# Seven-product projections that alternate between PSUM banks, with PSUM tiles of two banks, and attention transposes behind all value blocks

## The chip, the cores and the metric

The kernel runs on one core of one Trainium2 chip. The metric is the device time of one execution, in microseconds; lower is better. The engines are named as the profile names them: PE is TensorE (PEld its weight loads), ACT is ScalarE, DVE is VectorE, POOL is GpSimd, SP is SyncE, which here issues DMAs. PSUM, where products are summed, has banks of 512 fp32 values in each of 128 partitions.

## What is computed

One decoder layer in fp32 with D = 1024, 512 tokens and 16 meta tokens ahead of them (whose output is dropped). Two attention branches, retention with 4 heads and gated linear attention (GLA) with 4 heads, share one input projection, and sigmoid gates merge them:

```python
u = rms_norm(h, norm_gain)
proj = u @ w_in                      # 1024 x 11280 columns
(rq, rk, rv, rg, gq, gk, gv, gg, glr, m_ret, m_gla) = jnp.split(proj, points, axis=-1)
...
rq, rk = rope(rq), rope(rk) * 256 ** -0.5            # 4 heads of 256
o_ret = retention_chunked(rq, rk, rv)                # values: 4 heads of 512
o_ret = head_group_norm(o_ret, ret_norm_gain) * silu(rg)
...
o_gla = gla_chunked(gq, gk, gv, log_a)
o_gla = head_rms_norm(o_gla, gla_norm_gain) * silu(gg)
merged = sigmoid(m_ret) * (o_ret @ w_branch_ret) + sigmoid(m_gla) * (o_gla @ w_branch_gla)
return rms_norm(h + merged @ w_out, final_norm_gain)
```

(`rope` rotates the halves: `t1*cos - t2*sin` and `t2*cos + t1*sin`.)

## The kernel before

**Products.** Each fp32 operand is split in a rounded high part and the rest (`split`, lines 140 and 141: ACT casts to `hi`, DVE subtracts to `lo`), and each product is three matmuls: high by high, high by low, low by high. A weight is 512 x 256 in SBUF (`[128, 4, 256]`); its split has one cast on ACT and one subtraction on DVE. The splits lie in pools of three buffers each (`wsplit`).

**`quad`** computes two blocks of 256 columns of a projection from a 2 x 2 blocking with seven products in place of eight. The sums of activations (`fh`, `fl`, forms A11 to S4) are made once, those of weights at each quad on DVE (`tensor_sub` on `blk`, and `t2`). A product is 24 matmuls (2 halves, 4 pieces of 128, 3 parts). The products gather in three places, a, b and c. The order is 1 to b, 2 to a, 7 to c, then 6, 5 and 3 each added to b, then 4 to c. Bank b is copied by ACT to SBUF (`copy`, line 228) after product 1 (x1), after 6 (x2) and after 5 (x3), because the later products add to it; results are a + x1, c + x3, b, and c + x2. There are 21 quads. Those named `gq` and `rq` (query and key) are wide: the tokens with the meta tokens are the moving side, 264 columns for each half, so that a, b and c have two banks each. The others (`gg`, `gv1`, `rg`, `rv`, and the gates `mr`, `mg`) have 256 columns for each half and one bank each.

**PSUM.** Eight banks: pool `pp` with four tiles of one bank (b and c of the quads, the sums of branches and of the output), pool `pa` with four (a of the wide quads, attention, transposes).

**Evacuation.** The function `evac` that `quad` is given is called for each result; in wide quads for each of the two banks apart. For `rq` it applies `rope`: four multiplications on DVE, a subtraction and an addition on POOL (lines 757 to 762), and two splits.

**Attention of retention** (`ret_attention`): `values(ib)` for each block of 128 tokens computes a block of outputs `av` and norms it on DVE, POOL and ACT to gated rows `sg` (line 874). `turn` transposes `sg` on TensorE for two blocks at a time (line 337, tiles `ot`) and splits the result to `oh` (ACT) and `ol` (DVE). The order is values 0, 1, 2, turn 0, values 3, turn 1. `branch` multiplies `oh`, `ol` by the output weights (tiles `br_p`, eight sums of 512 columns, 12 matmuls each), each sum added to `acc2` by DVE.

**What sets the order.** The generators are woven: `weave(dense, chain)` advances the attention chain by one step after each product. Heads: `rq` of head h is woven with attention of head h-1, then comes the branch of head h-1, `rg` is woven with the scores, then `rv`. The gates are woven with attention of head 3. A scheduler then lays out each engine's instructions one after the other in one list, which need not be the order written; each engine goes through its list in order and waits at semaphores.

Of the kernel before, what the change touches and what calls it, by code (L numbers as in the profile page):

```python
# [106 lines left out]
def hybrid_kernel(ctx: ExitStack, tc: tile.TileContext, I, out: bass.AP):  # L107
# [6 lines left out]
    pp = ctx.enter_context(tc.tile_pool(name="pp", bufs=4, space=PSUM))  # L114
# [18 lines left out]
    def ppt(name):  # L133
        return pp.tile([P, 512], F32, tag="pp", name=name)
# [51 lines left out]
    def quad(cols, rows, name, evac, meta=None, wide=False):  # L186
# [13 lines left out]
        n_tok = HT if wide else 512  # L200
        banks = {}

        def bank(x):
            banks[x] = [(pat if wide and x == "a" else ppt)(f"{name}_{x}{t}") for t in range(2 if wide else 1)]

        def product(i, form, w, x, fresh):
            hi, lo = wsplit([P, 4, 256], f"{name}_{i}")
            split(hi, lo, w)
            if fresh:
                bank(x)  # L210
            for t in range(2):
                ps = banks[x][t][:, :HT] if wide else banks[x][0][:, t * 256:(t + 1) * 256]
                c = slice(t * P, (t + 1) * P)
                for kk in range(4):
                    a = [f[form][:, kk, c] if rows else f[form][:, kk, :HT if wide else 256] for f in (fh, fl)]
                    b = [f[:, kk, :] if rows else f[:, kk, c] for f in (hi, lo)]
                    first = fresh and kk == 0 and (wide or t == 0)
                    last = kk == 3
                    for j, (x1, x2) in enumerate(((0, 0), (0, 1), (1, 0))):
                        l, r = (a[x1], b[x2]) if rows else (b[x1], a[x2])  # L220
                        nc.tensor.matmul(ps, l, r, start=first and j == 0, stop=last and j == 2,  # L221
                                         skip_group_check=not fresh or (t == 1 and not wide))

        def copy(x, n):

            y = xc.tile([P, 2, HT] if wide else [P, 512], F32, tag="xc", name=f"{name}_x{n}")
            for t in range(2 if wide else 1):
                nc.scalar.copy(y[:, t, :] if wide else y, banks[x][t][:, :n_tok])  # L228
            return y

        def out(n, th, x, y):
            for t in range(2 if wide else 1):
                p = banks[x][t][:, :n_tok]
                q = y[:, t, :] if y is not None and wide else y
                evac(n, th, t if wide else None, p, q)
# [10 lines left out]
        x1 = copy("b", 1)  # L246
# [4 lines left out]
        nc.vector.tensor_sub(blk[0, 0], blk[0, 1], blk[0, 0])  # L251
# [30 lines left out]
    def proj_b(src, col, left, name, evac, meta=None):  # L282

        pss = [ppt(f"{name}_p{t}") for t in range(NTB)]
# [31 lines left out]
    def branch(src, row0, oh, ol, name, evac):  # L316
        for q in range(4):
# [3 lines left out]
            split(hi, lo, raw)  # L321
            for cc in range(2):
                c = 2 * q + cc
                ps = ppt(f"{name}_p{c}")
                for k in range(4):
                    mm3(ps, hi[:, k, cc * P:(cc + 1) * P], lo[:, k, cc * P:(cc + 1) * P], oh[:, k, :], ol[:, k, :],
                        k == 0, k == 3)
                evac(c, ps)
                yield
# [179 lines left out]
    def total(dst, p, q):  # L509
        if q is None:  # L510
            nc.scalar.copy(dst, p)
        else:
            nc.vector.tensor_add(dst, p, q)

    def pair(x):
        return x if x is None else x.rearrange("p (t c) -> p t c", t=2)

    def rows_into(dst, func=None):
        def f(n, th, t, p, q):
            d = dst[:, 2 * th:2 * th + 2, n * 256:(n + 1) * 256]  # L520
            if func is None:
                total(d, pair(p), pair(q))
                return
            if q is not None:
                total(d, pair(p), pair(q))
            nc.scalar.activation(d, pair(p) if q is None else d, func)
# [26 lines left out]
    def gla_qk(p):  # L553
# [4 lines left out]
        def evac(n, th, t, x, y):  # L558
            if n == 1:
                total(k[:, t, th, :], x, y)  # L560
            else:
                total(q[:, t, th * 256:(th + 1) * 256], x[:, :256], y if y is None else y[:, :256])
# [152 lines left out]
    def gla_branch(p):  # L715
        def evac(c, ps):
            if p == 0:
                nc.scalar.copy(acc[:, c, :], ps)
            else:
                nc.vector.tensor_add(acc[:, c, :], acc[:, c, :], ps)  # L720
                nc.sync.dma_start(kept[:, c, :], acc[:, c, :])
# [26 lines left out]

    def tmp(name):
        return rp.tile([P, 512], F32, tag="tmp", name=name, bufs=6)  # L750

    def rope(ts, th, dst, name):

        n = ts[0].shape[-1]
        co, si = cs[:, 0, th, :n], cs[:, 1, th, :n]
        m = [tmp(f"{name}_{i}")[:, :n] for i in range(4)]
        nc.vector.tensor_mul(m[0], ts[0], co)
        nc.vector.tensor_mul(m[1], ts[1], si)
        nc.gpsimd.tensor_sub(m[0], m[0], m[1])
        nc.vector.tensor_mul(m[2], ts[1], co)  # L760
        nc.vector.tensor_mul(m[3], ts[0], si)
        nc.gpsimd.tensor_add(m[2], m[2], m[3])
        for i in range(2):
            split(dst[0][i], dst[1][i], m[2 * i])

    def ret_qk(h):
# [5 lines left out]
        held = {}  # L772

        def evac(n, th, t, x, y):
            w = HT if n else 256
            if y is not None:
                s = tmp(f"qs{h}{n}{th}{t}")
                nc.vector.tensor_add(s[:, :w], x[:, :w], y[:, :w])
                x = s
            held[n, th, t] = x[:, :w]  # L780
            if t == 1:
                if n:
                    dst = [[f[:, i, th, :] for i in range(2)] for f in (kh, kl)]
                else:
                    dst = [[f[:, i, th * 256:(th + 1) * 256] for i in range(2)] for f in (qh, ql)]
                rope((held[n, th, 0], held[n, th, 1]), th, dst, f"rp{h}{n}{th}")
# [11 lines left out]
    def ret_v(h):  # L798
# [11 lines left out]
        def evac(n, th, t, x, y):  # L810
            x = pair(x)
            if y is not None:
                s = pair(tmp(f"vs{h}{n}{th}"))
                nc.vector.tensor_add(s, x, pair(y))
# [36 lines left out]
    def ret_attention(h):  # L851
# [39 lines left out]
    def gate(dst, n, th, p, q):  # L891
        if q is not None:
            nc.vector.tensor_add(dst, pair(p), pair(q))
        nc.scalar.activation(dst, pair(p) if q is None else dst, AF.Sigmoid)

    def gates():
# [3 lines left out]
        def evac_ret(j):  # L900
            def f(n, th, t, p, q):
                s = slice(th * 256, (th + 1) * 256)
                g = sigr[2 * j + n][:, :, s]
                gate(g, n, th, p, q)
# [4 lines left out]
        def evac_gla(j):  # L909
            def f(n, th, t, p, q):  # L910
                s = slice(th * 256, (th + 1) * 256)
                d = slice(4 * j + 2 * n, 4 * j + 2 * n + 2)
                k = pair(tmp(f"kp{j}{n}{th}"))
                nc.sync.dma_start(k, kept[:, d, s])
                g = pair(tmp(f"mg{j}{n}{th}"))
# [121 lines left out]
```

## Time and profile before

| | |
|---|---|
| time, median of 3 runs | 840.84 us (840.45 to 843.05) |
| the profiled execution | 841.58 us, its span 839.8 us |
| mean granted clock of TensorE | 0.988 |
| PE busy | 784.0 us (93%) |
| DVE busy | 619.5 us (74%) |
| ACT busy | 422.8 us (50%) |
| POOL busy | 133.7 us (16%) |
| DMA | 78.82 MB, mean 94 GB/s |

The span is the time from the first to the last instruction of the profiled execution; 1.8 us of its time lie around it. A matmul's record lasts longer than the distance to the next one, since matmuls are pipelined, so busy shares of PE overstate how well it is used: idle time is read from the waits and from the distance between starts.

### The profile page before, as it was taken

Reading aid. Unit: us, or ns where it says so; the run is one execution under the profiler, and the core shown is the slowest. Engines: PE = TensorE matmul, PEld = TensorE weight load, DVE = VectorE, ACT = ScalarE, POOL = GpSimd, SP = SyncE. Lnnn points to the kernel's source line nnn. Section 1 sums busy time; section 2 is a strip of 40 time slices with the busy share of each in tenths; the row PEclk is TensorE's granted clock in tenths of the full one; section 3 lists DMA queues with packets and bytes.
Section 4 is the critical chain, followed back from the end, with each engine's and each line's share of the span. In section 5 each row is a group of like instructions: output and inputs, shape, how many; then the busy total and the mean of one; then the engine's idle time right before and its main releaser. Section 6 shows DMA issues by size and latency. Waiting matters only on the chain. (4 is left out here: it accounts for less than half of the span.)

```text
span 839.8 us, 13348 instructions
## 1 busy us (share of the span) xinstructions
PE 784.0 (93%) x5322; PEld 703.9 (84%) x5322; DVE 619.5 (74%) x893; ACT 422.8 (50%) x707; POOL 133.7 (16%) x170
## 2 busy tenths in 40 slices
PE   7987989999899989999999999999999998989996
PEld 4777888898787978987999879998799998888886
DVE  3889686777637698887677887788877877887822
ACT  6665775456742445545445443454434555454422
POOL 4500332022400130022000220002200000032031
PEclk8998999999999999999999999999999999999999
DMA  8212211224122504242222422224222236335202
GB/s 278 84 56 76 76 45 54 66 90 126 52 75 100 177 25 127 77 125 75 69 81 79 126 76 64 81 83 127 76 64 82 82 105 208 114 103 176 73 1 101
DMA packets 72390, 78.82 MB, mean 94 GB/s; under 512 B 6964, under 2 KB 64564, under 8 KB 72328
## 3 DMA queue, kind: packets, MB, share of 16 engines
q1 hardware_dynamic: 72328, 77.97, 30.5%
q8 instruction: 42, 0.69, 0.3%
q14 instruction: 20, 0.16, 0.1%
HBM read 73.77 MB, written 4.19 MB: 93 GB/s over the span
## 5 line engine op out<-in xcount | busy, mean ns | idle before, releaser
L152 POOL TENSOR_TENSOR g_r<-g_v,mhalf 128x1 f32<-128x1 f32 x16 | 10.1, 630 | 305.7 <-DVE g_v L151 305.7
L144 PE MATMUL br_p<-oh,br_h 128*128 128x512 f32 x128 | 50.7, 401 | 1.0 <-ACT br_h L140 1.0
L145 PE MATMUL br_p<-ol,br_h 128*128 128x512 f32 x128 | 50.3, 396 | 0.0
L146 PE MATMUL br_p<-oh,br_l 128*128 128x512 f32 x128 | 50.1, 395 | 0.0
L140 ACT CAST rg_h<-rg_w 128x1024 fp32r<-128x1024 f32 x24 | 25.3, 1052 | 45.8 <-PE br_p L145 24.2
L140 ACT CAST rq_h<-rq_w 128x1024 fp32r<-128x1024 f32 x24 | 25.3, 1053 | 34.4 <-PE bg_p L145 13.0
L221 PE MATMUL rv_b<-rv_h,fh 128*128 128x256 f32 x128 | 37.0, 289 | 3.5 <-ACT rv_x L228 3.5
L221 PE MATMUL rq_b<-fh,rq_h 128*128 128x264 f32 x128 | 36.9, 288 | 1.0 <-ACT rq_x L228 1.0
L141 DVE TENSOR_TENSOR rg_l<-rg_w,rg_h 128x1024 fp32r<-128x1024 f32 x24 | 29.3, 1221 | 11.3 <-ACT rg_h L140 11.3
L221 PE MATMUL rg_b<-rg_h,fh 128*128 128x256 f32 x128 | 36.6, 286 | 0.9 <-DVE rp L760 0.9
L221 PE MATMUL rq_b<-fh,rq_l 128*128 128x264 f32 x128 | 36.6, 286 | 0.0
L221 PE MATMUL rq_b<-fl,rq_h 128*128 128x264 f32 x128 | 36.3, 283 | 0.0
L221 PE MATMUL rv_b<-rv_l,fh 128*128 128x256 f32 x128 | 36.0, 281 | 0.0
L221 PE MATMUL rg_b<-rg_l,fh 128*128 128x256 f32 x128 | 36.0, 281 | 0.0
L221 PE MATMUL rv_b<-rv_h,fl 128*128 128x256 f32 x128 | 36.0, 281 | 0.0
L221 PE MATMUL rg_b<-rg_h,fl 128*128 128x256 f32 x128 | 35.9, 281 | 0.0
L141 DVE TENSOR_TENSOR rv_l<-rv_w,rv_h 128x1024 fp32r<-128x1024 f32 x24 | 29.0, 1222 | 8.0 <-ACT rv_h L140 7.8
L141 DVE TENSOR_TENSOR rq_l<-rq_w,rq_h 128x1024 fp32r<-128x1024 f32 x24 | 30.4, 1266 | 3.9 <-ACT rq_h L140 3.9
L140 ACT CAST rv_h<-rv_w 128x1024 fp32r<-128x1024 f32 x24 | 24.8, 1053 | 12.2 <-DVE rv_w L252 5.6
L144 PEld LDWEIGHTS br_p<-oh,br_h 128*128 128x128 f32 x128 | 23.8, 188 | 8.2 <-ACT br_h L140 1.2
L221 PEld LDWEIGHTS rv_b<-rv_h,fh 128*128 128x128 f32 x128 | 24.1, 188 | 7.3 <-ACT rv_x L228 6.1
L145 PEld LDWEIGHTS br_p<-ol,br_h 128*128 128x128 f32 x128 | 24.1, 188 | 5.9
(478 smaller groups left out, 3062.1 us busy)
## 6 DMA issues: line engine op xcount, KB each, us to landing
rq_w<-in_w_in_dram SPq DMA_DIRECT2D x16, 512.0 KB, 3.7
rg_w<-in_w_in_dram SPq DMA_DIRECT2D x16, 512.0 KB, 3.6
rv_w<-in_w_in_dram SPq DMA_DIRECT2D x16, 512.0 KB, 3.7
br_w<-in_w_branch_ret_dram SPq DMA_DIRECT2D x16, 512.0 KB, 3.4
gv_w<-in_w_in_dram SPq DMA_DIRECT2D x8, 512.0 KB, 7.4
gq_w<-in_w_in_dram SPq DMA_DIRECT2D x8, 512.0 KB, 4.0
gg_w<-in_w_in_dram SPq DMA_DIRECT2D x8, 512.0 KB, 3.8
bg_w<-in_w_branch_gla_dram SPq DMA_DIRECT2D x8, 512.0 KB, 3.5
```

What stands on the lines that cost most here:

```text
L140: nc.scalar.copy(hi, src)
L141: eng.tensor_sub(lo, src, hi.bitcast(F32))
L144: nc.tensor.matmul(o, lh, rh, start=first, stop=False)
L145: nc.tensor.matmul(o, lh, rl, start=False, stop=False)
L146: nc.tensor.matmul(o, ll, rh, start=False, stop=last)
L152: nc.gpsimd.tensor_tensor(r[:rows], v[:rows], mhalf[:rows], op=ALU.pow)
L221: nc.tensor.matmul(ps, l, r, start=first and j == 0, stop=last and j == 2, skip_group_check=not fresh or (t == 1 and not wide))
```

## The change

1. `quad` takes the products in the order 1 (b), 2 (a), 6 (b), 7 (c), 5 (b), 4 (c), 3 (b). The copies are x1 of b after 1, x2 of b after 6, and x3 of c (in place of b) after 7; the results are a + x1, b + x3 after 5, c + x2 after 4, b after 3. The last product is 3 in place of 4. Weight sums are written in another order.
2. `pp` has two tiles of two banks. Quads that aren't wide have b and c in one tile and a in `pa`; wide ones have a tile each for b and c. Copies, sums, rope and the adding of branches handle both banks with one instruction. `rope` has two multiplications on DVE over 528 columns (cos and sin broadcast), two operations on POOL and one split. The branch's sums are added in pairs, and `kept` is written in four DMAs in place of eight. The pool `tmp` has five buffers of 528 columns in place of six of 512.
3. In `ret_attention` both turns follow all four value blocks.
4. The last output projection, `wo1`, has its sums in `pa`.

```diff
-    pp = ctx.enter_context(tc.tile_pool(name="pp", bufs=4, space=PSUM))
+    pp = ctx.enter_context(tc.tile_pool(name="pp", bufs=2, space=PSUM))
...
     def ppt(name):
-        return pp.tile([P, 512], F32, tag="pp", name=name)
+        return pp.tile([P, 2, 512], F32, tag="pp", name=name)
...
+        if wide:
+            c, b = ppt(f"{name}_c"), ppt(f"{name}_b")
+            a = [pat(f"{name}_a{t}") for t in range(2)]
...
+        else:
+            bc, a = ppt(f"{name}_bc"), pat(f"{name}_a")
...
         product(1, A11, blk[0, 0], "b", True)
-        x1 = copy("b", 1)
+        x1 = copy(b, 1)
...
         product(2, A12, blk[1, 0], "a", True)
         nc.vector.tensor_sub(blk[0, 0], blk[0, 1], blk[0, 0])
+        nc.vector.tensor_sub(t2, blk[1, 1], blk[0, 0])
+        evac(0, 0, a, x1)
+        yield
+        product(6, S2, t2, "b", False)
+        x2 = copy(b, 2)
         nc.vector.tensor_sub(blk[0, 1], blk[1, 1], blk[0, 1])
-        nc.vector.tensor_sub(t2, blk[1, 1], blk[0, 0])
-        out(0, 0, "a", x1)
         yield
         product(7, S3, blk[0, 1], "c", True)
-        yield
-        product(6, S2, t2, "b", False)
+        x3 = copy(c, 3)
         nc.vector.tensor_sub(blk[1, 0], blk[1, 0], t2)
-        x2 = copy("b", 2)
...
         product(5, S1, blk[0, 0], "b", False)
-        out(1, 1, "c", copy("b", 3))
+        evac(1, 1, b, x3)
         run_late()
         yield
+        product(4, A22, blk[1, 0], "c", False)
+        evac(0, 1, c, x2)
+        yield
         product(3, S4, blk[1, 1], "b", False)
-        out(1, 0, "b", None)
-        yield
-        product(4, A22, blk[1, 0], "c", False)
-        out(0, 1, "c", x2)
+        evac(1, 0, b, None)
         yield
...
-        m = [tmp(f"{name}_{i}")[:, :n] for i in range(4)]
-        nc.vector.tensor_mul(m[0], ts[0], co)
-        nc.vector.tensor_mul(m[1], ts[1], si)
-        nc.gpsimd.tensor_sub(m[0], m[0], m[1])
-        nc.vector.tensor_mul(m[2], ts[1], co)
-        nc.vector.tensor_mul(m[3], ts[0], si)
-        nc.gpsimd.tensor_add(m[2], m[2], m[3])
-        for i in range(2):
-            split(dst[0][i], dst[1][i], m[2 * i])
+        m = [tmpw(f"{name}_{i}")[:, :, :n] for i in range(2)]
+        nc.vector.tensor_mul(m[0], ts, co)
+        nc.vector.tensor_mul(m[1], ts, si)
+        nc.gpsimd.tensor_sub(m[0][:, 0, :], m[0][:, 0, :], m[1][:, 1, :])
+        nc.gpsimd.tensor_add(m[0][:, 1, :], m[0][:, 1, :], m[1][:, 0, :])
+        split(hi, lo, m[0])
...
-        values(0)
-        yield
-        values(1)
-        yield
-        values(2)
-        yield
-        turn(sg, 0, oh, ol, rgain, h * 4, f"ot{h}")
-        yield
-        values(3)
-        yield
-        turn(sg, 1, oh, ol, rgain, h * 4, f"ot{h}")
-        yield
+        for ib in range(NTB):
+            values(ib)
+            yield
+        for half in range(2):
+            turn(sg, half, oh, ol, rgain, h * 4, f"ot{h}")
+            yield
```

How the instructions stand in an engine's list, before and after, at three places. The first is TensorE in the value projection of head 0, where product 5 ends and `rq` of head 1 comes next (`rv_5_h` is the cast of product 5's weights, `rq_1_h` that of the next quad's first product). Before:

```order
L221 MATMUL rv_b_3458<-rv_5_h,fh_83 128x256
L221 MATMUL rv_b_3458<-rv_5_l,fh_83 128x256
L221 MATMUL rv_b_3458<-rv_5_h,fl_90 128x256
L221 MATMUL rv_b_3458<-rv_3_h,fh_86 128x256
L221 MATMUL rv_b_3458<-rv_3_l,fh_86 128x256
L221 MATMUL rv_b_3458<-rv_3_h,fl_93 128x256
```

After:

```order
L226 MATMUL rv_bc<-rv_5_h,fh_83 128x256
L226 MATMUL rv_bc<-rv_5_l,fh_83 128x256
L226 MATMUL rv_bc<-rv_5_h,fl_90 128x256
L226 MATMUL rq_b<-fh_80,rq_1_h 128x264
L226 MATMUL rq_b<-fl_87,rq_1_h 128x264
L226 MATMUL rv_bc<-rv_4_h,fh_82 128x256
L226 MATMUL rv_bc<-rv_4_l,fh_82 128x256
```

Product 4 now follows product 5, and between them stand two matmuls of the next quad's product 1.

The second is ScalarE at the boundary of the gate quads mg0 and mg1 (`mg_4_h` and `mg_3_h` are casts for mg0's products 4 and 3, `mg_1_h` and `mg_2_h` for the first two of mg1, `mg_x` the copies x2 and x3, line 894 or 889 the sigmoids). Before, from mg0's cast for product 4:

```order
L140 CAST mg_4_h<-mg_w_7607 128x1024
L228 COPY mg_x_7742<-mg_b_7617 128x512
L140 CAST mg_1_h<-mg_w_7850 128x1024
L228 COPY mg_x_7772<-mg_b_7617 128x512
L894 ACTIVATE mg_7776<-mg_7776 128x512
L140 CAST mg_2_h<-mg_w_7852 128x1024
```

After, from mg0's cast for product 4:

```order
L141 CAST mg_4_h<-mg_w_7396 128x1024
L232 COPY mg_x_7500<-mg_bc 128x512
L141 CAST mg_3_h<-mg_w_7400 128x1024
L232 COPY mg_x_7531<-mg_bc 128x512
L141 CAST mg_1_h<-mg_w_7638 128x1024
L889 ACTIVATE mg_7564<-mg_7564 128x512
```

Before, the cast for mg1's product 1 stands between the two copies, which are both of bank b; after, the two copies are of the two banks of `mg_bc`, and that cast stands behind both.

The third is VectorE at the end of `rq` of head 2, woven with attention of head 1 (`ol` are the splits of the turned rows, `rp` the rope, `sg` the gated rows, `b`, `mv`, `nm` the norm of the last value block). Before:

```order
L867 BN_STATS b_5102<-av_5088 128x6
L868 BN_AGGR mv_5103<-b_5102 128x2
L151 TENSOR_SCALAR g_v<-mv_5103 128x1
L871 SCALAR_TENSOR_TENSOR nm_5110<-mv_5103,g_r 128x1
L757 TENSOR_TENSOR rp_0_5143<-rq_b_4813,cs 128x264
L758 TENSOR_TENSOR rp_1_5144<-rq_b_4814,cs 128x264
L874 TENSOR_TENSOR sg_4252<-on_5112,sg_4252 128x512
L760 TENSOR_TENSOR rp_2_5145<-rq_b_4814,cs 128x264
L761 TENSOR_TENSOR rp_3_5146<-rq_b_4813,cs 128x264
L141 TENSOR_TENSOR kl_4800<-rp_0_5143,kh_4799 128x264
L345 SCALAR_TENSOR_TENSOR ol_4843<-ot_10_5157,rgain,oh_4842 128x256
L345 SCALAR_TENSOR_TENSOR ol_4843<-ot_11_5166,rgain,oh_4842 128x256
```

After:

```order
L344 SCALAR_TENSOR_TENSOR ol_4723<-ot_00_4956,rgain,oh_4722 128x256
L344 SCALAR_TENSOR_TENSOR ol_4723<-ot_01_4965,rgain,oh_4722 128x256
L517 TENSOR_TENSOR qs_5002<-rq_c,rq_x_4833 128x2x256
L344 SCALAR_TENSOR_TENSOR ol_4723<-ot_10_5012,rgain,oh_4722 128x256
L767 TENSOR_TENSOR rp_0_5004<-qs_5002,cs 128x2x256
L768 TENSOR_TENSOR rp_1_5005<-qs_5002,cs 128x2x256
L344 SCALAR_TENSOR_TENSOR ol_4723<-ot_10_5012,rgain,oh_4722 128x256
L344 SCALAR_TENSOR_TENSOR ol_4723<-ot_11_5021,rgain,oh_4722 128x256
L767 TENSOR_TENSOR rp_0_5058<-rq_b,cs 128x528
L142 TENSOR_TENSOR ql_4677<-rp_0_5004,qh_4676 128x2x256
L344 SCALAR_TENSOR_TENSOR ol_4723<-ot_11_5021,rgain,oh_4722 128x256
L768 TENSOR_TENSOR rp_1_5059<-rq_b,cs 128x528
```

The norm and the gating of block 3 are gone from this place, the `ol` of turn 1 stand among the sums and the rope of the last two products, and the very last `ol` stands behind `ql` of the query's second half.

More of the change, by code (lines that the diff above doesn't have):

```diff
@@ L199, in quad @@
                                   .rearrange("(k p) c -> p k c", p=P))
[L200 to L204, printed above, removed]
+        if wide:
+            c, b = ppt(f"{name}_c"), ppt(f"{name}_b")
+            a = [pat(f"{name}_a{t}") for t in range(2)]
+            banks = {"a": [x[:, :HT] for x in a], "b": [b[:, t, :HT] for t in range(2)],
+                     "c": [c[:, t, :HT] for t in range(2)]}
+            b, c = b[:, :, :HT], c[:, :, :HT]
+        else:
+            bc, a = ppt(f"{name}_bc"), pat(f"{name}_a")
+            banks = {x: [y[:, t * 256:(t + 1) * 256] for t in range(2)]
+                     for x, y in (("a", a), ("b", bc[:, 0, :]), ("c", bc[:, 1, :]))}
+            a, b, c = [x.rearrange("p (t c) -> p t c", t=2) for x in (a, bc[:, 0, :], bc[:, 1, :])]
         def product(i, form, w, x, fresh):
@@ L771, in ret_qk, with evac @@
         R["qk", h] = qh, ql, kh, kl
-        held = {}
-        def evac(n, th, t, x, y):
+        def evac(n, th, x, y):
             w = HT if n else 256
             if y is not None:
-                s = tmp(f"qs{h}{n}{th}{t}")
-                nc.vector.tensor_add(s[:, :w], x[:, :w], y[:, :w])
+                s = tmpw(f"qs{h}{n}{th}")[:, :, :w]
+                total(s, x, y)
                 x = s
[L780 to L786, printed above, removed]
+            hi, lo = [f[:, :, th, :] for f in (kh, kl)] if n else \
+                     [f[:, :, th * 256:(th + 1) * 256] for f in (qh, ql)]
+            rope(x[:, :, :w], th, hi, lo, f"rp{h}{n}{th}")
         yield from quad((C_RQ + h * 256, C_RK + h * 256), False, f"rq{h}", evac, wide=True)
```

126 lines of the change are left out of this document (65 added, 61 removed).

## Prediction

> **What bounds the kernel now.** I read the busy shares first, then the waits of TensorE, then the chain of waits in one stage, and last the timelines around the waits that the change touches. The page's first line:
>
> ```profile
> PE 784.0 (93%) x5322; PEld 703.9 (84%) x5322; DVE 619.5 (74%) x893; ACT 422.8 (50%) x707; POOL 133.7 (16%) x170
> ```
>
> TensorE carries the span, and the change leaves its products as they are. So only TensorE's idle time can be won. The list of its waits (total us, times, longest us) names who ends it:
>
> ```profile
> PE ot L337 <- DVE sg L874: 10.1, 7, 1.8
> PE gq_b L221 <- DVE gq_l L141: 5.1, 1, 5.1
> PE rv_b L221 <- ACT rv_x L228: 3.5, 8, 0.7
> PE mg_b L221 <- ACT mg_x L228: 3.1, 2, 1.6
> PE mg_b L221 <- ACT mg_h L140: 2.1, 2, 1.1
> PE mr_b L221 <- ACT mr_x L228: 1.9, 2, 1.5
> ...
> PE sc L144 <- ACT qh L140: 1.3, 1, 1.3
> ...
> PE rq_b L221 <- ACT rq_x L228: 1.0, 1, 1.0
> ...
> PE rg_b L221 <- DVE rp L760: 0.9, 1, 0.9
> ...
> PE gq_b L221 <- ACT gq_x L228: 0.4, 1, 0.4
> ```
>
> Two kinds stand out: transposes `ot` waiting for the gated rows `sg`, and a product on bank b waiting for ScalarE's copy `x` of that bank or for the cast `h` of its weights. These rows count from the modelled end of the last matmul. Here is what one such wait costs:
>
> ```profile
> 446.46 0.39 PE L221 MATMUL rv_b<-rv_h,fh 128*128 128x256 f32 x1 [0.21 <-ACT rv_x L228]
> ...
> 449.29 0.28 PE L221 MATMUL rv_b<-rv_h,fl 128*128 128x256 f32 x1
> 450.25 0.39 PE L221 MATMUL rv_b<-rv_h,fh 128*128 128x256 f32 x1 [0.68 <-ACT rv_x L228]
> ```
>
> From 449.29 to 450.25 are 0.96 us. Matmuls in a row follow each other by 0.12 (24 in 2.84 us, in the chain below), so 0.84 are lost where the row says 0.68. Each wait is worth 0.16 more than its row.
>
> **The gates.** The chain of waits in mg0 (start, duration, what), and ScalarE's timeline there:
>
> ```profile
> 728.68 2.74 PE mg_b L221 x23
> ...
> 731.61 0.84 issue
> 732.45 0.59 ACT mg_x L228
> ...
> 733.08 2.99 PE mg_b L221 x23
> ...
> 736.10 1.05 ACT mg_h L140
> ...
> 737.20 3.58 PE mg_b L221 x26
> 740.78 2.84 PE mg_c L221 x24
> ```
>
> ```profile
> 731.50 1.04 ACT L140 CAST mg_h<-mg_w 128x1024 fp32r<-128x1024 f32 x1 [1.80 <-PE mg_b L221]
> 732.45 0.58 ACT L228 COPY mg_x<-mg_b 128x512 f32<-128x512 f32 x1
> ```
>
> Product 6 ends at 731.42. ScalarE first makes the cast for product 4, which had waited for product 6 to free its buffer, then copies b (x2), and product 5 begins at 733.08: 1.66 us lost. Product 5 ends at 736.07. In TensorE's list two matmuls of the next quad's product 1 come next, whose cast waits for the buffer of product 5; at 737.20 these two and product 3 (26) go on: 1.13 more. After the change every copy has a whole product (2.84) between itself and the next write of its bank, and the copy behind a cast takes 1.05 + 0.59. Eight matmuls of the next product 1 stand behind product 4, so product 4 covers their cast. Both losses go in three quads (mr1, mg0, mg1): 3 x 2.79 = 8.4. mr0's own first copies (as in rv above, 0.21 + 0.16 and 0.84) give 1.2. Together **+9.6**; by the wait rows alone it would be 3.1 + 2.1 + 1.9 = 7.1, the lower end.
>
> **The value projections.** The eight copies are covered: +3.5. But the order shows that two matmuls of the next quad's first product now follow product 5 directly. Their cast waits for the buffer of product 5 itself, the pattern of 736.07 to 737.20: 1.13 in each of four heads, -4.5. **Net -1.0** (+3.5 if the cast finds a free buffer, -3 if the copies still wait). Besides, product 3 now comes last and holds block 0 of the values. VectorE's rows at this place before:
>
> ```profile
> 452.92 1.22 DVE L251 TENSOR_TENSOR rq_w<-rq_w,rq_w 128x1024 f32<-128x1024 f32 x1
> 454.05 0.68 DVE L141 TENSOR_TENSOR vl<-rv_b,vh 128x512 fp32r<-128x512 f32 x1
> ```
>
> The last `vl` stands behind such weight subtractions. One of 1.22 is half covered by the 2.9 us of the next product: 0.5 a head, **-2.0** (0 to -6).
>
> **The transposes.** TensorE, then VectorE, in head 1:
>
> ```profile
> 369.46 0.87 PE L337 MATMUL ot<-ident,sg 128*128 128x128 f32 x6 [1.35 <-DVE sg L874]
> ...
> 383.03 0.87 PE L337 MATMUL ot<-ident,sg 128*128 128x128 f32 x6 [1.74 <-DVE sg L874]
> ```
>
> ```profile
> 378.95 0.69 DVE L867 BATCH_NORM_STATS2 b<-av 128x6 f32<-128x512 f32 x1
> ...
> 381.77 1.21 DVE L874 TENSOR_TENSOR sg<-on,sg 128x512 f32<-128x512 f32 x1 [0.23 <-ACT on L873]
> ```
>
> From the statistics of block 3 to its `sg` are 4.0 us, and before only one product of 2.9 (24 x 0.122) lies between block 3 and its transposes. After, turn 0 stands behind product 5, with three products since block 1, and turn 1 behind product 4, with two products (5.9) since block 3. 5.9 covers 4.0 and leaves 1.9 for a queue on VectorE. The waits go: **+10.1** (5 if VectorE's queue is worse than that).
>
> What is late next is the branch. The last `oh` and `ol` of turn 1 now stand behind product 3's rope, behind the casts of `br_2` and of q. Rows by group (us busy, mean ns), and the pace of branch matmuls:
>
> ```profile
> 769.78 0.24 PE br_p L144
> ```
>
> ```profile
> L345 DVE SCALAR_TENSOR_TENSOR ol<-ot,rgain,oh 128x256 fp32r<-128x256 f32 x32 | 14.0, 478 | 1.4 <-ACT oh L344 0.9
> ...
> L759 POOL TENSOR_TENSOR rp<-rp,rp 128x264 f32<-128x264 f32 x8 | 10.8, 1346 | 30.8 <-DVE rp L758 30.8
> ...
> L140 ACT CAST vh<-vs 128x512 fp32r<-128x512 f32 x12 | 7.4, 620 | 0.3 <-DVE vs L814 0.3
> ...
> L759 POOL TENSOR_TENSOR rp<-rp,rp 128x256 f32<-128x256 f32 x8 | 6.7, 835 | 21.8 <-DVE rp L758 21.8
> ...
> L814 DVE TENSOR_TENSOR vs<-rv_c,rv_x 128x512 f32<-128x512 f32 x8 | 5.5, 687 | 0.1
> ```
>
> Counted from product 4's end: sum and two rope multiplications 3 x 0.69, one `ol` between 0.48, two POOL operations of 0.84: 4.2, that is 1.3 after product 3's end. Then q's cast 0.62, `ql` 0.69, the last `ol` 0.48 and some 0.4 of hand-overs: 3.5. The branch needs it after nine matmuls of 0.235, 2.1. So it stands 1.4, or 2.4 if POOL takes 1.35 as for 264 columns. I take 1.7 in three heads: **-5.1** (-1 to -8).
>
> **Head 0.** TensorE at the start of rg0:
>
> ```profile
> 298.07 0.39 PE L221 MATMUL rg_b<-rg_h,fh 128*128 128x256 f32 x1 [0.85 <-DVE rp L760]
> ...
> 302.60 0.91 PE L144 MATMUL sc<-qh,kh 128*128 128x512 f32 x4 [1.30 <-ACT qh L140]
> ```
>
> The waits of `rq_b` (1.0) and `rg_b` (0.9) go with the pairs of banks: **+1.9**. The first scores now need the keys of product 3, the last: two rope multiplications, two POOL operations, cast and subtraction, 2 x 0.69 + 2 x 0.84 + 0.62 + 0.69 = 4.4, to which VectorE adds `ql` in between, and one product and one matmul of cover (3.0) as before: with hand-overs some 3 more than now. Such a wait can cost twice, as the windows show (us, busy time of PE, PEld, DVE, ACT, POOL, then granted clock):
>
> ```profile
> 62.71:66.12 3.41, 0.96 (x8) 0.75 (x7) 3.41 (x8) 1.15 (x2) 0.00 (x0) 1.00 0.00 0
> 66.12:69.54 3.42, 0.81 (x3) 0.81 (x4) 3.42 (x5) 2.85 (x2) 0.00 (x0) 0.50 0.00 0
> 346.00:384.50 38.50, 35.41 (x264) 33.67 (x262) 33.40 (x63) 19.48 (x33) 8.12 (x10) 1.00 0.32 96
> ```
>
> After 3.41 us with TensorE busy for 0.96, the next 3.42 were granted half the clock, 1.7 us if it were full of work. I add 1.0 for that: **-4.0** (-1 to -6). The Trainium skill, "TensorE: Matmul & The Clock Gate", section "What's actually happening", says that one idle window of about 3.4 us halves the clock; the two windows agree.
>
> **The rest.** gq's copy wait: **+0.4**. gq0's 5.1 stays: its releaser is VectorE, behind the forget gates, which the change leaves (±2). Halving the number of VectorE's evacuations saves fixed time there, but in stages where VectorE isn't last: 0, except that it makes the queue shorter in 346 to 384.5, where it is busy for 33.4 of 38.5. Four DMAs fewer for `kept`: 0, since no row of TensorE's waits names them. wo1's sums in the other pool: 0 (-1), since nothing else uses that pool by then. Start-to-start surplus: 7 + 8 + 2 removed waits outside the gates, less about 8 new ones, of 0.16: **+1.4**. Pairs instead of single banks in the pool: each pair is read within a product: 0 (-2).
>
> **Sum:** 9.6 - 1.0 - 2.0 + 10.1 - 5.1 + 1.9 - 4.0 + 0.4 + 1.4 = 11.3. The profiled execution took 841.6 (839.8 of span and 1.8 around it), 0.7 above the median of 840.8. So 840.8 - 11.3 = **829.5**.
>
> **Rivals.** *VectorE's order eats the gain.* It is 87% busy in the heads, and each stall that goes compresses its work. Then half of the transposes' 10.1 stays, the branch costs 8, the first scores 6: 829.5 + 5 + 3 + 2 = 839.5. For it speaks that before, VectorE was often the last; against, that it gets shorter by the pairs. Chance 0.12, within 0.3% of before (2.5 us, about what a measurement here can tell from no change).
> *Slower: the branch's first tile becomes a stall with half clock.* If the last `ol` of turn 1 comes 5 us late instead of 1.7, TensorE stands for a window, then runs a window at half: 3 x (3.3 + 1.7) = 15 more, **844.5**. It decides from some 4.6 us a head, (11.3 + 2.5) / 3, in all. For it: three engines hand on in sequence behind product 3; against: the rows give 3.5 us for that chain, and TensorE works through 2.1 of them. Chance 0.07.
> *All stalls go:* branch 0, the casts of the next quad find a buffer, the first scores wait as now: 829.5 - 5.1 - 4.5 - 3 = 817, chance 0.08; half of that, 823, lies in the range of my case.
> *Pairing delays.* An instruction on two banks releases its first half as late as its second, by one single, about 0.4 us, where the consumer waits: branch and first scores or first values, 2 places in 4 heads, 3.2: 832.7. In the profile, ScalarE is busy for half the span and yet ends waits, which speaks for it; that most pairs feed work a product later speaks against. Chance 0.18. The Trainium skill, "Perfetto Trace Analysis", section "Optimizing Scalar/DVE Operations", says it as a rule: where these engines aren't saturated but make bubbles on others, breaking instructions up may let work finish sooner. That is against this change; the copies of 0.59 that come late behind casts of 1.05 rather show the order than the size as the cause.
>
> **How the numbers follow.** My case, 0.55, at 829.5, from 822 to 836 by its own bounds. With the others, 0.18 at 833, 0.12 at 839.5, 0.08 at 817 and 0.07 at 844.5, I set the range from 820 to 840: below it 0.08, above it 0.12. Faster by over 0.3% (below 838.3): 0.55 + 0.18 + 0.08 and a quarter of 0.12, 0.84; within 0.3%: 0.09; slower: 0.07.
>
> **What would show it.** In the trace after: no `ot` waits on `sg` in the heads (transposes right); no copy `x` among TensorE's waits, and none over 0.3 between the gates' quads; new waits of `rq_b` or `mr_b` of about 1.1 behind product 5 on a cast (value projections); branch matmuls waiting on `ol` or `oh` for 1 to 2.5; `sc` waiting for 4 in head 0, perhaps with a half clock. I am wrong above all if TensorE's new waits on `ol` are longer than that, or if VectorE's queue makes the transposes late all the same.

## Result: 869.6 us, 3.4% slower

The changed kernel takes 869.58 us (median, 869.41 to 870.52), the kernel before 841.15 us in the same comparison: ratio 1.0336, 95% interval 1.0318 to 1.0355. Forecast were 829.5 us and a range of 820 to 840. The profiled execution took 869.5 us, with a span of 867.7.

The first line of the page, TensorE's granted clock in 40 slices, and the list of TensorE's waits in the changed kernel (total us, times, longest us):

```profile
PE 796.6 (92%) x5322; PEld 709.7 (82%) x5322; DVE 607.2 (70%) x821; ACT 417.5 (48%) x665; POOL 142.7 (16%) x170
...
PEclk8999999999999989999999999999899999999999
```

```profile
PE br_p L145 <- DVE qs L517: 10.1, 3, 3.4
PE sc L145 <- ACT kh L141: 7.4, 1, 7.4
PE mg_bc L226 <- ACT mg_x L232: 6.7, 4, 2.0
PE rv_bc L226 <- ACT rv_x L232: 3.7, 8, 0.7
PE rq_b L226 <- ACT rq_h L141: 3.4, 3, 1.1
...
PE mr_bc L226 <- ACT mr_x L232: 2.2, 2, 1.5
...
PE br_p L146 <- DVE ol L344: 1.8, 3, 0.6
PE mg_bc L226 <- DVE mg L517: 1.7, 2, 0.9
```

VectorE and ScalarE have less to do than before, TensorE has the same 5322 matmuls, and the span is 28 us longer: the loss is idle time, and matmuls at half the clock. The waits of `ot` on `sg` (10.1 us) are gone. The waits on the copies `x`, which the new order should have ended, are not: 6.7 in the gates mg (3.1 before), 2.2 in mr (1.9) and 3.7 in the value projections (3.5); in the wide quads gq, they grew from 0.4 to 3.6. New are the branch's first sum, waiting for the query's sum, and a long wait of the first scores.

**Why a copy of b still stops product 7.** TensorE and ScalarE in rv of head 0. Product 6 into b ends with the matmul of 342.51; the next is product 7 into c:

```profile
342.51 0.28 PE L226 MATMUL rv_bc<-rv_h,fl 128*128 128x256 f32 x1
343.46 0.39 PE L226 MATMUL rv_bc<-rv_h,fh 128*128 128x256 f32 x1 [0.68 <-ACT rv_x L232]
```

```profile
342.82 0.58 ACT L232 COPY rv_x<-rv_bc 128x512 f32<-128x512 f32 x1 [1.21 <-PE rv_bc L226]
```

The copy reads bank b, the product writes bank c, and yet the product starts 0.06 us after the copy's end (343.40). Both banks belong to one tile, `rv_bc`, and the program makes the writer of the tile wait for its reader, whichever bank each of them uses. So the new order's alternation is undone where b and c are halves of a tile: in all quads but the wide ones. That the shared tile is the cause is tested below, by giving b and c different tiles.

**The branch and the first scores.** TensorE at the end of rq of head 1, VectorE there, and two windows (us, busy time of PE, PEld, DVE, ACT, POOL, then granted clock):

```profile
387.38 0.28 PE L226 MATMUL rq_b<-fh,rq_l 128*128 128x264 f32 x1
391.03 0.47 PE L145 MATMUL br_p<-oh,br_h 128*128 128x512 f32 x1 [3.37 <-DVE qs L517]
...
392.93 0.80 PE L146 MATMUL br_p<-ol,br_h 128*128 128x512 f32 x1 [0.59 <-DVE ol L344]
```

```profile
388.80 0.71 DVE L142 TENSOR_TENSOR kl<-rp,kh 128x528 fp32r<-128x528 f32 x1 [1.30 <-ACT kh L141]
389.42 0.87 DVE L344 SCALAR_TENSOR_TENSOR ol<-ot,rgain,oh 128x256 fp32r<-128x256 f32 x2
390.21 0.68 DVE L517 TENSOR_TENSOR qs<-rq_c,rq_x 128x512 f32<-128x512 f32 x1
```

```profile
389.40:392.80 3.40, 1.31 (x4) 0.67 (x4) 3.40 (x9) 2.82 (x5) 0.18 (x1) 1.00 0.39 132
392.80:396.20 3.40, 3.27 (x7) 2.11 (x8) 2.55 (x6) 0.99 (x2) 1.25 (x2) 0.52 0.00 0
```

The branch's first sum needs the pair of banks that product 4 of rq filled, and VectorE reads it (`qs`) only at 390.21, behind `kl`, which had waited 1.30 for a cast, and two `ol`. 3.5 us go, then TensorE has half the clock. In head 0 the first scores start 7.4 us late, and the clock halves too:

```profile
307.07 0.79 PE L145 MATMUL sc<-qh,kh 128*128 128x512 f32 x1 [7.38 <-ACT kh L141]
```

```profile
304.00:307.40 3.40, 0.33 (x1) 0.33 (x2) 2.07 (x3) 1.01 (x2) 2.67 (x3) 0.53 0.00 0
307.40:310.80 3.40, 3.40 (x15) 3.21 (x15) 2.65 (x3) 1.61 (x2) 2.87 (x4) 0.50 0.00 0
```

The spans by part (us; the last two kernels are from the experiments). Each part is cut where its matmuls begin behind the last one of the part before; in the changed kernel 18 matmuls of the first gate quad, 2.2 us, already stand among the heads. The row of e5_ac is from the quickest run of that kernel, 6 us below its median:

| | up to rq of head 0 | heads 0 to 3 | gates | last branch and output |
|---|---|---|---|---|
| before | 275.2 | 391.0 | 100.7 | 73.0 |
| changed | 275.7 | 413.9 | 105.3 | 72.8 |
| changed, a and c share (e5_ac) | 271.7 | 389.4 | 95.0 | 74.1 |
| order alone (e1_order) | 271.6 | 390.1 | 92.4 | 73.8 |

### The profile page after: what moved, and what is told of

Its sections match the earlier page's. It is cut to its first block, busy times and chain, and to the rows that moved or that the text cites. A ratio compares the mean times of both kernels' runs of the same rounds, so it can differ in the third digit from the quotient of the medians.

```text
span 867.7 us, 13199 instructions
## 1 busy us (share of the span) xinstructions
PE 796.6 (92%) x5322; PEld 709.7 (82%) x5322; DVE 607.2 (70%) x821; ACT 417.5 (48%) x665; POOL 142.7 (16%) x170
## 5 line engine op out<-in xcount | busy, mean ns | idle before, releaser
L145 PE MATMUL br_p<-oh,br_h 128*128 128x512 f32 x128 | 52.4, 411 | 10.1 <-DVE qs L517 10.1
L226 PE MATMUL rv_bc<-rv_h,fh 128*128 128x256 f32 x192 | 55.3, 288 | 3.7 <-ACT rv_x L232 3.7
L226 PE MATMUL rg_bc<-rg_h,fh 128*128 128x256 f32 x192 | 55.5, 289 | 0.1
L226 PE MATMUL rv_bc<-rv_l,fh 128*128 128x256 f32 x192 | 54.0, 281 | 0.0
L226 PE MATMUL rg_bc<-rg_l,fh 128*128 128x256 f32 x192 | 54.0, 281 | 0.0
L226 PE MATMUL rv_bc<-rv_h,fl 128*128 128x256 f32 x192 | 53.9, 281 | 0.0
L226 PE MATMUL rg_bc<-rg_h,fl 128*128 128x256 f32 x192 | 53.8, 280 | 0.0
L226 PEld LDWEIGHTS rv_bc<-rv_h,fh 128*128 128x128 f32 x192 | 36.1, 188 | 8.0 <-ACT rv_x L232 6.3
L141 ACT CAST rg_h<-rg_w 128x1024 fp32r<-128x1024 f32 x24 | 25.3, 1052 | 31.2 <-PE br_p L146 13.2
L145 PEld LDWEIGHTS br_p<-oh,br_h 128*128 128x128 f32 x128 | 25.1, 196 | 18.2 <-ACT oh L343 12.5
L226 PEld LDWEIGHTS rg_bc<-rg_h,fh 128*128 128x128 f32 x192 | 36.1, 188 | 4.4 <-issue 1.6
L142 DVE TENSOR_TENSOR rv_l<-rv_w,rv_h 128x1024 fp32r<-128x1024 f32 x24 | 29.0, 1221 | 10.6 <-ACT rv_h L141 10.6
L226 PEld LDWEIGHTS rv_bc<-rv_h,fl 128*128 128x128 f32 x192 | 36.2, 189 | 0.0
L226 PEld LDWEIGHTS rg_bc<-rg_h,fl 128*128 128x128 f32 x192 | 36.2, 189 | 0.0
```

What stands on the lines that cost most here:

```text
L141: nc.scalar.copy(hi, src)
L142: eng.tensor_sub(lo, src, hi.bitcast(F32))
L145: nc.tensor.matmul(o, lh, rh, start=first, stop=False)
L226: nc.tensor.matmul(ps, l, r, start=first and j == 0, stop=kk == 3 and j == 2, skip_group_check=not fresh or (t == 1 and not wide))
```

## Experiments

The edits fall in three: the order of products, the late turns, and the pairs. The first four runs take them apart; times are medians, and ratios are to the kernel before, 841.1 us.

**Order of products alone**: the `quad` of before, with the products and copies of the changed kernel on single banks.

```diff
+        product(6, S2, t2, "b", False)
+        x2 = copy("b", 2)
...
         product(7, S3, blk[0, 1], "c", True)
...
-        product(6, S2, t2, "b", False)
+        x3 = copy("c", 3)
...
-        x2 = copy("b", 2)
...
         product(5, S1, blk[0, 0], "b", False)
-        out(1, 1, "c", copy("b", 3))
+        out(1, 1, "b", x3)
...
+        product(4, A22, blk[1, 0], "c", False)
+        out(0, 1, "c", x2)
...
         product(3, S4, blk[1, 1], "b", False)
         out(1, 0, "b", None)
...
-        product(4, A22, blk[1, 0], "c", False)
-        out(0, 1, "c", x2)
```

> The kernel before with the new order of the seven products alone (single banks, old order of the transposes). Theory A (in the changed kernel b and c share one tile, and a product into c waits for the copy or sum that reads b; the order itself is good): the copies x2 and x3 leave TensorE's waits, the gates win about 9 us, the value projections 3 to 5, rq of head 0 about 1: 826 to 829 us. Theory B (the order itself makes the last evacuations late, whatever the tiles): no gain or a loss, 840 to 850 us.

829.46 us, ratio 0.986 (0.9825 to 0.9895): theory A, 0.5 us above what it expected. Of the waits on copies one row is left, gq's:

```profile
PE ot L338 <- DVE sg L875: 12.2, 7, 2.2
PE sc L144 <- ACT kh L140: 5.0, 4, 2.1
...
PE gq_b L221 <- ACT gq_x L228: 0.4, 1, 0.4
```

**Late turns alone**: the kernel before, with the loop over `values` and then both turns, as in the diff of the change.

> The kernel before with both turns behind all four value blocks, nothing else. Theory A: the waits of the transposes (10.1 us) go, the branch waits some 1 to 2 us a head for the last rows: 833 to 837 us. Theory B, here that turning late starves the branch (in the changed kernel the branch stands 3.5 us for its first sum and 2.5 more right behind it in each of three heads): 850 to 858 us.

840.13 us, ratio 0.9982 (0.9968 to 0.9996): neither theory. The `ot` waits are gone, and the same time stands elsewhere:

```profile
PE br_p L144 <- DVE rp L760: 3.9, 3, 1.4
...
PE rq_b L221 <- ACT rq_x L228: 3.3, 4, 1.3
...
PE br_p L144 <- ACT oh L344: 2.1, 3, 0.7
```

**Both, on single banks.**

> The kernel before with the new order of products and both turns last, single banks and single evacuations. Theory A: both gains together, 820 to 825 us. Theory B: as slow as the changed kernel or nearly, 855 to 870 us.

839.29 us, 0.997 (0.9957 to 0.9984): neither. The late turns cost 9.8 us on top of the order. Its waits, and three windows at the start of a branch (columns as above):

```profile
PE sc L144 <- ACT kh L140: 11.1, 4, 3.3
...
PE br_p L145 <- DVE ol L346: 3.6, 3, 1.2
PE br_p L144 <- ACT oh L345: 3.6, 3, 1.2
```

```profile
375.20:378.60 3.40, 2.14 (x4) 1.01 (x4) 2.75 (x8) 1.56 (x5) 1.86 (x2) 0.68 0.03 5
378.60:382.00 3.40, 0.79 (x2) 0.70 (x3) 3.20 (x8) 1.76 (x4) 1.49 (x2) 0.50 0.00 0
382.00:385.40 3.40, 3.40 (x9) 2.63 (x9) 3.40 (x5) 0.33 (x1) 3.01 (x4) 0.50 0.21 43
```

**Pairs alone**: the changed kernel with the old order of products and of turns.

> The changed kernel with the old order of products and the old order of the transposes, so that the pairs of banks and the instructions on pairs are left of the change. Theory A: the pairs are the loss, 855 to 865 us, with waits of products into c on what reads b, and of the branch's first sum on the query's sum. Theory B: near the kernel before, 838 to 846 us.

872.31 us, 1.0356 (1.0331 to 1.0382): the pairs are the loss, 31 us, more than the 14 to 24 expected. Which part of them? The next four edits of the changed kernel ask.

**a and c share the tile instead of b and c.**

```diff
-            bc, a = ppt(f"{name}_bc"), pat(f"{name}_a")
+            ac, b = ppt(f"{name}_ac"), pat(f"{name}_b")
...
-                     for x, y in (("a", a), ("b", bc[:, 0, :]), ("c", bc[:, 1, :]))}
+                     for x, y in (("a", ac[:, 0, :]), ("b", b), ("c", ac[:, 1, :]))}
...
```

> The changed kernel, but in the quads that aren't wide a and c share the tile of two banks, and b has a bank of its own in the other pool; instructions and orders are otherwise as in the changed kernel. Theory A1 (the loss is that b and c share a tile, so that a product into c waits for the copy or sum that reads b, and the other way round): the gates and the value projections come down to the order-alone kernel's, 848 to 856 us, and the waits on x in gates and values go. Theory A2 (the loss is the paired rope, whose longer chain starves scores and branch): 863 to 868 us.

837.93 us (831.95 to 840.07), 0.9951 (0.9925 to 0.9976). This kernel varies more than the others: its granted clock was 0.979 in the quickest run, which is the one in the trace, and 0.969 in the slowest. 31.7 us come back, more than the 14 to 22 that theory A1 expected. TensorE and ScalarE at the place shown above, product 6 and then product 7:

```profile
335.91 0.28 PE L226 MATMUL rv_b<-rv_h,fl 128*128 128x256 f32 x1
336.03 0.27 PE L226 MATMUL rv_ac<-rv_h,fh 128*128 128x256 f32 x1
```

```profile
336.23 0.59 ACT L232 COPY rv_x<-rv_b 128x512 f32<-128x512 f32 x1 [1.22 <-PE rv_b L226]
```

Product 7 follows in 0.12 us, and the copy runs beside it. Part of the surplus is in the lists, which came out otherwise: no two matmuls of the next quad stand behind product 5 any more (in the changed kernel, 3.4 us of waits on `rq_h` and 1.1 on `mr_h`). By the table above, 4.0 us more came back ahead of rq of head 0. The rest of the surplus isn't taken apart.

**The branch's first two sums in single banks of the other pool.**

```diff
-            ps = ppt(f"{name}_p{q}")
+            if q == 0 and name[:2] == "br":
+                ps = [pat(f"{name}_p{q}{cc}") for cc in range(2)]
+            else:
+                ps = ppt(f"{name}_p{q}")
...
```

> The changed kernel, but the first two sums of each retention branch lie in two single banks of the other pool and are added one by one, so that the branch's first sum needs no pair that the query's sum has to free. Theory A3 (that wait, 10.1 us in three heads, and the half clock behind it are lost to the pairs in the branch): 856 to 861 us. The rival, that the rows ol are as late anyway: the wait turns into one on ol a few matmuls later, 865 to 869 us.

868.78 us, 1.0327 (1.03 to 1.0354): the rival. Given banks, the branch waits for the rows:

```profile
PE br_p L145 <- ACT oh L346: 8.5, 3, 2.8
```

**Rope in single instructions, on the pairs of banks.**

```diff
-        nc.vector.tensor_mul(m[0], ts, co)
-        nc.vector.tensor_mul(m[1], ts, si)
+        nc.vector.tensor_mul(m[0][:, 0, :], ts[:, 0, :], co)
+        nc.vector.tensor_mul(m[0][:, 1, :], ts[:, 1, :], si)
...
+        nc.vector.tensor_mul(m[1][:, 0, :], ts[:, 1, :], co)
+        nc.vector.tensor_mul(m[1][:, 1, :], ts[:, 0, :], si)
...
```

> The changed kernel with rope in single instructions again (four multiplications on VectorE over 256 or 264 columns, two operations on POOL, two splits), on the same pairs of banks. Theory A2 (the paired rope lengthens the chain to the keys and queries: the first scores of head 0 wait 7.4 us, the branch 3.4): 850 to 857 us, with the wait of the first scores at 1 to 3 us. Theory A1: 866 to 872 us, that wait hardly shorter, since POOL's time is set by VectorE's work beside it.

876.44 us, 1.0422 (1.0399 to 1.0445): 7 us slower than the changed kernel, so A2 falls; it is slower than A1 expected, too. Scores now wait in every head:

```profile
PE sc L145 <- ACT kh L141: 18.2, 4, 5.2
```

**The changed kernel with the old turns.**

> The changed kernel with the old order of the transposes (pairs and the new order of products are left). If order and pairs simply add (-11.6 for the order, +31.2 for the pairs against the kernel before): 860 us. Theory A1 (the shared tile takes the order's gain away): 868 to 876 us.

870.55 us, 1.0348 (1.0325 to 1.0371): against the pairs alone (872.3) the new order brings 1.8 of its 11.6 us. A1: the shared tile takes the order's gain away.

**a and c share, old turns.**

> The changed kernel with a and c in the shared tile (as in the run before that had it, 837.9 us) and with the old order of the transposes besides. Theory T (behind the new order of products the late turns cost more than their waits were worth, since oh and ol and the keys of the last product come to the branch and the scores together): 826 to 831 us, near the order alone (829.5), with some 10 us of ot waits back and shorter waits of the branch. Rival (the late turns are harmless where the tiles are right): 842 to 848 us, since the ot waits come back.

841.3 us, 0.9998 (0.9988 to 1.0008), just below the rival's 842: theory T fails on the pairs, where the late turns gain 3.4 us. The transposes' waits came back, 12.0 us. From the last product's last matmul to the next quad, the branch takes 24.2 to 25.8 us in place of 27.5 to 27.8, so it wins back only 6.9 in three heads; it now waits for `ol` alone:

```profile
PE ot L336 <- DVE sg L875: 12.0, 7, 2.3
PE br_p L146 <- DVE ol L344: 6.1, 3, 2.0
```

**Pairs alone, no two sums in a tile.** In the kernel of the pairs alone, for quads that aren't wide:

```diff
-            bc, a = ppt(f"{name}_bc"), pat(f"{name}_a")
+            b, c, a = ppt(f"{name}_b")[:, 0, :], pat(f"{name}_c"), pat(f"{name}_a")
...
```

> The pairs alone (old orders of products and of transposes, 872.3 us), but in quads that aren't wide c has a single bank of the other pool and b a tile for itself, so that no two sums share a tile. Theory A1 (the shared tile is the loss of the pairs): back to the kernel before, 836 to 846 us. Rival (instructions on two banks and the fewer, larger tiles cost by themselves): 855 to 865 us.

861.19 us, 1.0243 (1.0228 to 1.0258): the rival. With the old order the shared tile costs 11.1 us, and the pairs 20 more by themselves. 9.5 of these stand in the rq and rg of head 0 (63.7 us from the first matmul of rq to that of rv, 54.2 before), 6.2 in the rq of heads 1 to 3 and 2.1 in the branches behind them. The long waits in head 0, which were 1.3 us on `qh` and 1.0 on `rq_x` before:

```profile
PE sc L145 <- ACT qh L141: 7.1, 1, 7.1
...
PE rq_b L225 <- ACT rq_x L231: 4.7, 2, 3.3
```

The wait of 3.3 in ScalarE's list:

```profile
289.77 0.62 ACT L141 CAST qh<-rp 128x512 fp32r<-128x512 f32 x1 [3.11 <-POOL rp L768]
290.29 1.04 ACT L141 CAST rq_h<-rq_w 128x1024 fp32r<-128x1024 f32 x1
291.24 0.59 ACT L231 COPY rq_x<-rq_b 128x528 f32<-128x528 f32 x1
```

The copy that product 5 needs is one instruction on both banks, behind a cast of weights and one cast of both halves of the query, which waits for POOL to finish both. TensorE goes on at 291.88. In the kernel before, the copy of the first bank (0.37 us) stands ahead of that cast of weights, product 5 begins right behind it, and TensorE waits 1.0. So the first half is released as late as the second, as in the prediction's rival "Pairing delays".

**a and c share, and value block 2 a step earlier.**

```diff
-        for ib in range(NTB):
-            values(ib)
-            yield
-        for half in range(2):
-            turn(sg, half, oh, ol, rgain, h * 4, f"ot{h}")
-            yield
+        values(0)
+        yield
+        values(1)
+        values(2)
+        yield
+        values(3)
+        yield
+        turn(sg, 0, oh, ol, rgain, h * 4, f"ot{h}")
+        yield
+        turn(sg, 1, oh, ol, rgain, h * 4, f"ot{h}")
+        yield
```

> As the kernel with a and c shared (837.9 us), but with value block 2 a step earlier, so that each turn comes one product earlier than in the changed kernel (values 0; 1 and 2; 3; turn 0; turn 1). Theory T: the branch finds oh and ol earlier and waits less, while three products still lie behind block 3: 824 to 831 us. Rival (VectorE's queue at the end of rq is the limit, wherever the turns stand): 836 to 842 us.

827.31 us, 0.9842 (0.9826 to 0.9858): as theory T expected, and the fastest of all, 10.6 us below the same kernel with the late turns. Neither `oh` nor `ol` is waited for in the branch any more; a cast of its weights is:

```profile
PE br_p L145 <- ACT br_h L141: 7.0, 3, 2.4
PE sc L145 <- ACT kh L141: 5.8, 1, 5.8
```

**b and c share again in the gates alone** (`if name[0] == "m"`).

> The kernel with a and c shared (837.9 us), but in the four gate quads b and c share the tile again, as in the changed kernel. If the shared tile's 31.7 us are made by the waits where they stand (gates mr1 to mg1 some 10 us by the two traces), this costs 9 to 12 us: 847 to 850 us. Rival (the loss is made elsewhere, in the heads, and the gates only follow): 838 to 842 us.

846.59 us, 1.0057 (1.0036 to 1.0078): 8.7 us above the kernel with a and c shared, just below the 9 to 12 expected, with the same waits as in the changed kernel:

```profile
PE mg_pair L229 <- ACT mg_x L235: 6.7, 4, 2.0
```

In the two traces the gates take 110.3 and 95.0 us, 15.3 apart, the second from that kernel's quickest run. So the loss is made where the waits stand: 9 to 15 in the gates, the rest in the heads and ahead of them.

**Scores of heads 1 to 3 in the branch's pool**, on single banks with order and late turns.

```diff
-            ps = pat(f"sc{h}{jb}")
+            ps = (ppt if h else pat)(f"sc{h}{jb}")
```

> New order of products and late turns on single banks (839.3 us), but the scores of heads 1 to 3 have their sums in the pool that the branch's sums also use, so that no score can stand in TensorE's list ahead of the branch's matmuls. Theory H (late turns lost on top of the order because the list puts a score matmul among the branch's first matmuls, which waits up to 3.3 us for the keys, and the clock halves behind it): 826 to 832 us, with the branch at 23 to 26 us in place of 31. Rival (oh and ol are too late for the branch in any case): 836 to 842 us.

843.13 us, 1.0023 (1.0008 to 1.0038), just above the rival's 842: theory H falls. No score stands among the branch's first matmuls, and the branch is as long (30.2 to 30.8 us; 30.1 to 31.2 with them), waiting for banks and rows:

```profile
PE br_p L144 <- DVE rp L761: 7.2, 3, 2.7
...
PE br_p L145 <- DVE ol L346: 3.6, 3, 1.2
PE br_p L144 <- ACT oh L345: 3.6, 3, 1.2
```

**The same with value block 2 a step earlier.**

> The same scores' pool, single banks and the new order of products, with value block 2 a step earlier (values 0; 1 and 2; 3; turn 0; turn 1). If single instructions are no worse than pairs: 820 to 827 us, below the paired kernel with the same steps (827.3). If pairs are worth something by themselves: 828 to 833 us.

839.83 us, 0.9975 (0.9962 to 0.9988): neither. On single banks the list begins four sums of the branch at once (four pairs of `oh` and `ol` on `br_h` stand ahead of the first matmul on `br_l`), and their banks wait for product 3's rope:

```profile
PE br_p L144 <- DVE rp L761: 11.9, 3, 4.0
```

The paired kernel with the same steps works through one sum at a time and is 12.5 us faster. The scores' pool differs as well, which cost 3.8 us with the late turns; the early step on single banks with the scores left in place wasn't run.

The runs by order, turns and tiles in one table (median us):

| products | turns | single banks | pairs, b and c share | pairs, no such sharing |
|---|---|---|---|---|
| old | old | 841.1 | 872.3 | 861.2 |
| new | old | 829.5 | 870.6 | 841.3 (a, c) |
| old | late | 840.1 | | |
| new | late | 839.3 | 869.6 (the change) | 837.9 (a, c) |
| new | a step earlier | 839.8 (scores moved) | | 827.3 (a, c) |

## Why the prediction was wrong, step by step

- **The gates, +9.6.** The mechanism and its size hold on single banks: 100.7 to 92.4 us, 8.3. In the changed kernel the gates got 4.6 us longer, though 2.2 us of their work had moved ahead of them. What failed is the step "every copy has a whole product (2.84) between itself and the next write of its bank". That is true of the bank, but the wait is for the tile. It counted the cover by banks and never asked what the program orders by, though b and c in one tile were named as part of the change.
- **The value projections, -1.0 and -2.0.** The inserted matmuls of the next quad came as read from the order: three waits of 1.1 on `rq_h` and one on `mr_h`. The +3.5 for the copies didn't come (3.7 us are still waited), for the same reason. The -2.0 for the late `vl` isn't seen: no row of TensorE waits for it.
- **"Pairs instead of single banks in the pool: each pair is read within a product: 0 (-2)"** is the worst term: 31.7 us through the shared tile. The pair of rq that the branch needs, which product 4 filled, was read only from 390.21 on, some 2.5 us after the end of the product that came next, not within it.
- **The transposes, +10.1.** Their waits went. But the branch, priced at 5.1, lost 17.3 in three heads: from the last product's last matmul to the next quad it takes 28.2 to 29.6 us, 22.9 before. 3.5 in each go ahead of the first sum, the rest behind it, at half the clock. The chain to the last `ol` was priced without VectorE's queue: in the trace `kl` ahead of it had waited 1.30 for a cast, itself behind a POOL operation of 1.73. On single banks the late turns are worth 1.0 us in the old order and cost 9.8 in the new one; I had +5.0.
- **Head 0, +1.9 and -4.0.** rq went from 22.9 to 21.0 us, the 1.9 forecast. rg, with the first scores, went from 31.3 to 37.3, so 6.0 lost where 4.0 were forecast, with the half clock that the trace shows. The mechanism is right, the size of the wait was not: 7.4 us where some 4 were expected.
- **gq, +0.4.** The copies' waits there grew to 3.6 us. These quads share no tile, but there, too, one copy handles both banks.
- **The rivals.** The slower one put its price on the branch with half the clock. The half clock was seen in each head, but behind a wait for banks, not for `ol`; and the 12.2 us that the branch lost beyond the 5.1 forecast are less than a third of the 40 between forecast and result. *Pairing delays* named a mechanism that the runs show, but priced it at 3.2 us: on unshared pairs it and what comes with it are 20 in the old orders. No rival held the shared tile. The rule of the Trainium skill, "Perfetto Trace Analysis", section "Optimizing Scalar/DVE Operations", that breaking instructions up may let work finish sooner, was weighed with that rival. The runs show both: breaking up the rope alone made the changed kernel 7 us slower, while with the old orders the kernel with single instructions throughout is 20 us faster than the one with unshared pairs.
- **The half clock** was forecast from two windows, in which TensorE was not idle but busy for 0.96 and 0.81 us; the last section gives the bound that all traces show.

Without the shared tile the change is worth -3.1 us, not -11.3. The three edits don't add: the order gains 11.6, and then either the turns (9.8 on single banks) or the pairs (11.8 with the old turns) eat most of it, though the second of the two costs nothing more. What the pairs cost by themselves (20 us with both old orders, 12 with the new products and old turns, within 2 of nothing with both new) is measured, but its mechanism is seen only in head 0, not proved for the rest. Why late turns gain on pairs and lose on single banks behind the new order is shown as far as the branch goes: with them its time, from the last product on, rises from 25.0 to between 31.5 and 32.7 us on single banks (about 1 of it the work of scores), where the list begins several sums and scores that all wait, and by 1.6 to 3.3 on pairs, where it works through one sum at a time. The waits of `ot` that they save are about 12 us in both. What makes the lists come out so stays open.

## To carry to other kernels

In this program, alternating between banks hid an evacuation only where the banks belonged to different tiles, the unit by which it orders accesses: ask what each writer waits for before counting what lies between. When banks are joined for wider instructions, join those whose reads and writes don't alternate; here a and c, not b and c. A wait taken away by moving work later isn't a gain until the next consumer has been priced with the whole queue of the engines that feed it.

## What the runs showed that was not expected

The granted clock changes on a grid of 3.41 us in these traces, and a window's clock goes with how long TensorE was busy, by its rows, in the one before. Over the sixteen traces, each of the 93 windows at full clock with 1.53 us of busy time or less was followed by one at half the clock; of the 144 with 1.54 to 2.20, 18 were; of the 3539 with more, none. From half the clock the step is sharper: all 51 windows with less than 2.9 us of busy time were followed by another at half, and none of the 101 with more. So a wait of 2.0 us was enough in two of the three branches of the kernel with a and c shared and old turns. By estimate, from the length of a window, each one at half the clock costs up to 1.7 us more; behind the branch's wait in head 2 of the changed kernel there were two in a row, and that branch took some 1.3 us longer than the other two.

Three edits that each removed a real wait (late turns, banks for the branch's first sum, the scores' pool) moved the time by -1.0, -0.8 and +3.8 us: on a chain that three engines feed, the next wait was there each time.
